# The next block's x is cast in pairs 2 to 5 in place of 0 to 3, and the first two differences of g become one

## The chip, the cores and the metric

One Trainium2 chip, one core of it. The metric is the device time of one execution in microseconds; the median of several runs is compared. TensorE (PE, with its weight loads PEld), VectorE (DVE), ScalarE (ACT), GpSimd (POOL) and SyncE (SP, which here only issues DMAs) each run their own instructions in order, and wait for each other through semaphores. DMAs are issued from two queues: SP's, and GpSimd's own, which also does the transfers that convert a type.

## The reference

```python
def reference(x, w1, w2):          # x 8x1024x1024, w1 1024x4096, w2 4096x1024, float32
    h = x @ w1
    h = 0.5 * h * (1 + np.tanh(np.sqrt(2 / np.pi) * (h + 0.044715 * h ** 3)))
    return (h @ w2).astype(np.float32)
```

## The kernel before, in words

The 8192 tokens are worked through in eight blocks of 1024 (`sb`, 0 to 7). Each block has a first matmul (x times w1, then GELU, which gives g) and a second (g times w2). All operands are float16, and the sums are float32 in PSUM. Both matmuls use a fast scheme of seven products in place of eight: an operand is cut into four blocks "11", "12", "21", "22", sums and differences of the blocks are formed, seven products are made of them (numbers 1 to 7), and their results are added. In blocks 2 to 7 the scheme is used on two levels, so that most products are themselves made of seven smaller ones. This leaves TensorE less to do and VectorE more.

**The first matmul of blocks 2 to 7** is `matmul1_late`. For a block of x, "21" is the second token half and the first half of the hidden dimension. The loop over `j` from 0 to 7 makes one *pair* after another: two chunks of 128 intermediate columns, in each half of g. The four tiles of g are g["11"], g["12"], g["21"] and g["22"], each 128 x 16 x 512, of which pair j fills chunks 2j and 2j + 1. What is done in a pair, and in which order, stands in the list `PAIR` (and `PAIR_FIRST`, `PAIR_LAST`). Every key is one step: `m` and `h` are matmuls (lines 723 and 509), `a`, `p`, `c` copies by ScalarE (line 179), `e`, `f`, `s`, `u`, `z` additions by VectorE (line 152), `g` a GELU by ScalarE (line 522). A key with a prime belongs to the pair before. So the end of pair j - 1 is worked out in pair j, and `d'`, which stands near the end of the list, is step d of the pair before.

- **Step d** (lines 525 to 530 and 769 to 771) replaces g["21"] by g["11"] - g["21"] in the two chunks of its pair: 128 x 1024 float16 values, in place. It runs on GpSimd in pairs 0 to 6 and on VectorE in pair 7 (line 528). What it makes is read in the second matmul.
- **The sums of x** that the inner products need are made on VectorE in float16 (line 368, at line 152 in the profile): at the steps `i` of `PAIR_FIRST`, and in pair 1 at the steps that `X_SUMS` names; the last of these, `i64`, comes after the last key of the list. There are none in later pairs.
- **The weights of a pair** are a `StoredHalf`: six groups (`GROUPS`) that SP loads from DRAM (line 305), as far ahead as the 26 buffers of the pool `up` allow; two halves are there at the start of the stage, and half j + 2 is asked for in pair j. Of halves 3 to 7 the group (s1, s5) isn't loaded; GpSimd makes it in four operations (`make`, line 330) from the group (1, 5), and this stands in GpSimd's order at the start of the pair before.
- **The next block's x** is first converted from float32 to float16, from DRAM to DRAM, into `xb`: `x_cast_paced` (lines 487 to 492). It issues a copy of two columns into a tile `pace` on GpSimd (line 489, called the mark), which waits for a chunk of g and so holds back what follows it, and then two DMAs of 128 rows each on GpSimd's queue (line 484). One call is called a cast pair here. Four of them convert the 1024 rows.
- **Then x is transposed** into four blocks by `x_transpose` (lines 494 to 504): four transposing DMAs a block on SP's queue (`DMA_TRANSPOSE`, line 176), in the order "22", "21", "12", "11", at the ends of pairs 4, 5, 6 and 7. The first two blocks hold the second token half (rows 512 to 1023), the last two the first.

Behind the third transposed block SP issues the first three weight loads of the second matmul (`early.load`, line 815), then the fourth block, then the rest of the second matmul's weights (lines 1011 and 1015). The second matmul's own matmuls have line 1030. At the end of pair 5 GpSimd makes one sum for it (`early.make`, line 1024, 128 x 2048). In its course GpSimd's queue stores the output (line 840).

Blocks 0 and 1 have other code (`matmul1`, `matmul2_made`), which calls `difference` too, on VectorE.

Of the kernel before, what the change touches and what calls it, by code (L numbers as in the profile page):

```python
# [88 lines left out]
def kernel(  # L89
# [7 lines left out]
    nc = tc.nc  # L97
# [10 lines left out]
    NI = I // P // 2  # L108
# [36 lines left out]
    def temp():  # L145
        return tp.tile([P, HT], F32, name="tmp")
# [31 lines left out]
    def act_copy(out, in_):  # L178
        tc.keep_in_program_order(nc.scalar.copy(out=out, in_=in_))  # L179
# [190 lines left out]
    def x_blocks():  # L370
        return {b: unit(KH, HT) for b in ("22", "21", "12", "11")}
# [107 lines left out]
    def x_cast(s, after, rows=range(0, SB, P), xb=None):  # L479
        if xb is None:  # L480
            xb = xdram.tile([SB, H], DT, name="xb")
        with tc.issue_after(after.ins):
            for q in rows:
                nc.gpsimd.dma_start(out=xb[q:q + P, :], in_=x2[s * SB + q:s * SB + q + P, :])
        return xb

    def x_cast_paced(s, g_chunk, q, xb, pin=False):

        mark = nc.gpsimd.tensor_copy(out=pace, in_=g_chunk[:, :2])
        if pin:  # L490
            tc.keep_in_program_order(mark)
        return x_cast(s, mark, range(q * P, (q + 2) * P, P), xb)

    def x_transpose(xb, dma, blocks=None, which=range(4)):
        blocks = blocks or x_blocks()
        for b, t in [list(blocks.items())[i] for i in which]:
            a, k = int(b[0]) - 1, int(b[1]) - 1
            for j in range(KH):
                dma(
                    t[:, j, :],  # L500
                    xb[a * HT:(a + 1) * HT, (k * KH + j) * P:(k * KH + j + 1) * P],
                    transpose=True,
                )
        return blocks
# [13 lines left out]
    def add(out, in1, in0=None):  # L518
        tt(out, out if in0 is None else in0, in1, ADD, True)

    def gelu_into(out, src):
        gelu_last[0] = nc.scalar.activation(out=out, in_=src, func=GELU)  # L522
        tc.keep_in_program_order(gelu_last[0])

    def difference(g, j, engine=nc.vector):
        if j >= 0:
            cs = slice(2 * j, 2 * j + 2)
            tc.keep_in_program_order(engine.tensor_tensor(  # L528
                out=g["21"][:, cs], in0=g["11"][:, cs], in1=g["21"][:, cs], op=SUB,
            ))  # L530
# [4 lines left out]
    def g_tiles():  # L535
        return {b: g_tile(b) for b in ("11", "12", "21", "22")}
# [6 lines left out]
    def matmul1(xs, sb, quads, start=None):  # L543
# [29 lines left out]
        for j in range(NI // 2):  # L573
# [46 lines left out]
            for h in range(2):  # L620
                add(a[h], banks_b[h])
            difference(g, j - 1)
            half = (len(jobs) + 1) // 2
            if start is not None and j == 1:
# [56 lines left out]
    class Pair:  # L681
# [7 lines left out]
        def bank(self, b, h):  # L689
            if (b, h) not in self.banks:  # L690
                self.banks[b, h] = psum()
            return self.banks[b, h]
# [35 lines left out]
        def run(self, key):  # L728
            kind, m, i = key[0], int(key[1:2] or 0), int(key[2:3] or 0)
            bank, temp = self.bank, self.temp  # L730
            if kind == "m" and m in self.whole:
                if i in (1, 4):
                    self.half(m, int(i == 4), m != 6)
            elif kind == "m":
                self.part(m, i)
            elif kind == "h":
                self.half(m, i, False)
            elif kind in "czf" and m in self.whole:
                pass
            elif kind == "c":  # L740
                act_copy(temp("c", m)[:, left], bank("a" if m == 1 else "c", 1)[:, right])
            elif kind == "z" and m in (1, 5):
                b = "a" if m == 1 else "c"
                z = bank(b, 1)[:, left]
                if i == 1:
                    act_copy(bank(b, 0)[:, left], z)
                else:
                    out = bank(b, 0) if i == 2 else bank(b, 1)
                    add(out[:, right], z, temp("c", m)[:, left])
            elif kind == "f":  # L750
                add(temp("q", 0)[:, right if i else left], bank("a", 1)[:, right], temp("a", i)[:, right])
            elif kind in "ez":
                b, t = {2: ("b", "a"), 3: ("d", "s"), 6: ("a", "a")}[m]
                z = bank(b, 1)[:, left]
                if kind == "e":
                    add(temp(t, i)[:, right], bank(b, 1)[:, right])
                else:
                    h, cols = ((0, left), (0, right), (1, right), (1, left))[i - 1]
                    base = temp(t, h)[:, cols]
                    if m == 6 and cols == right:  # L760
                        base = temp("q", 0)[:, right if h else left]
                    add(bank(b, h)[:, cols], z, base)
            elif kind in "ap":
                act_copy(temp(kind, m), bank("a" if kind == "a" else "c", m))
            elif kind == "s":
                add(temp("s", m), bank("a", m), temp("p", m))
            elif kind == "u":
                add(temp("p", m), bank("a", m))
            elif kind == "d":
                spare = self.j < NI // 2 - 1  # L770
                difference(self.g, self.j, nc.gpsimd if spare else nc.vector)
            else:
                b, h = key[1:3], int(key[3])
                src = temp("p", h) if b == "22" else bank({"11": "b", "21": "a", "12": "d"}[b], h)
                gelu_into(self.g[b][:, 2 * self.j + h, :], src)

    def matmul1_late(xs, sb, quads, g):
        n = NI // 2
        nxt = {}
        early = Inner(4, g["22"])  # L780
        made = set(xs.inner)

        def x_sum(key):
            if int(key[1]) not in made:
                xs.inner_sum(int(key[1]), int(key[2]))

        last = None
        for j in range(n + 1):
            if MADE_HALF <= j + 1 < n:
                quads[j + 1].make()  # L790
            if j < n:
                quads += [StoredHalf(i) for i in range(len(quads), min(j + 3, n))]
                now = Pair(j, quads[j], xs, g)
            if j == n:
                for key in PAIR_LAST:
                    last.run(key)
                break
            for key in PAIR if j else PAIR_FIRST:
                if key[0] == "i":
                    x_sum(key)  # L800
                elif key[-1] == "'":
                    last.run(key[:-1])
                else:
                    now.run(key)
                for job in X_SUMS.get(key, ()) if j == 1 else ():
                    x_sum(job)
            last = now
            if sb < NSB - 1:
                if j < 4:
                    after = g["11"][:, 2 * j - 1, :] if j else xs.inner[5][:, 0, 0, :]  # L810
                    nxt["xb"] = x_cast_paced(sb + 1, after, 2 * j, nxt.get("xb"), True)
                if j == 3:
                    nxt["blocks"] = x_blocks()
                if j == n - 1:
                    early.load(STEPS[:3])
                if j > 3:
                    x_transpose(nxt["xb"], load_in_order, nxt["blocks"], range(j - 4, j - 3))
            if j == 5:
                early.make(7, nc.gpsimd, up, "u")
        blocks = nxt.get("blocks")  # L820
        return g, early, None if blocks is None else XOps(blocks)
# [261 lines left out]
    def matmul2(sb, g, early, nxt):  # L1083
# [56 lines left out]
        new, quads = {}, []  # L1140
        products[4].load()
        run((0, 0))
        for m, after in zip(order, order[1:] + (None,)):
            into[m] = into[1] if m == 6 else [claim(), claim()]
# [23 lines left out]
    xs, quads = first.xs, [first.quad]  # L1168
    g_late = None
    for sb in range(NSB):  # L1170
        if sb < 2:
            g, nxt = matmul1(xs, sb, quads, first if sb == 0 else None)
            xs, quads = matmul2_made(sb, g, None if sb else quads[-1].keep_raw, nxt)
            continue
        g, early, nxt = matmul1_late(xs, sb, quads, g_late or g_tiles())
        g_late, quads = matmul2(sb, g, early, nxt)
        xs = nxt
# [30 lines left out]
```

## Time and profile before

| | us |
|---|---|
| median of 3 runs | 1480.92 |
| lowest and highest of them | 1478.4, 1481.01 |
| the profiled execution | 1483.45 |
| its span, from the first to the last instruction | 1481.7 |

The profile is of one execution. In its views a line of a group or of a timeline names the line of the code, the engine, the operation, and the tiles as out<-in; in square brackets, or behind the bar, stands how long the engine was idle before it and what ended that. `ps` is a PSUM bank, `tmp` a float32 tile that ScalarE or VectorE fills from PSUM, `u` and `gc` are tiles of the two pools that hold weights and sums, `g` is g, `w_d` and `in_d` are the prepared weights in DRAM. The wait view has total time, number of times, and the longest. The view of one line or tile ends with how long its DMAs took from issue to landing. Times on GpSimd are rough.

### The profile page before, as it was taken

To read this page: it belongs to the slowest core of one execution; us is meant where nothing else is said; L and a number is where in the kernel's file an instruction comes from. 1 tells how busy PE (TensorE), PEld (TensorE's weight loads), DVE (VectorE), ACT (ScalarE), POOL (GpSimd) and SP (SyncE) were. 2 spreads that over 40 slices of the span, in tenths; PEclk is the share of its full clock that TensorE was granted. 3 is DMA by queue.
4 is the path that set the end of the run, shared out by engine and by line. 5 is a ranking of instruction groups with operands and counts; after the bars stand their busy time and mean duration, and the time that the engine had idled before them with its cause. 6 is when DMAs were issued, how large, how long until landed. Compare 5 with 4: busy or idle time off the path is not lost.

```text
span 1481.7 us, 28425 instructions
## 1 busy us (share of the span) xinstructions
PE 1457.0 (98%) x10635; PEld 1039.1 (70%) x10635; DVE 1264.3 (85%) x2226; ACT 611.1 (41%) x1226; POOL 454.9 (31%) x473
## 2 busy tenths in 40 slices
PE   9999999999989999999999999999999999999998
PEld 5444444444467888678877788777886778867787
DVE  5657468768789999999999999999999999899997
ACT  5665125621157411663126621366214752056510
POOL 1442122223347012560026501274103631136111
PEclk9999999999999999999999999999999999999999
DMA  9999897898999999999999999999999999996896
GB/s 324 338 337 391 234 345 278 309 289 286 362 346 220 349 291 365 352 221 364 302 370 329 211 379 316 363 293 231 383 340 343 290 281 324 352 338 215 319 295 220
DMA packets 205706, 462.86 MB, mean 312 GB/s; under 512 B 75648, under 2 KB 80768, under 8 KB 204672
## 3 DMA queue, kind: packets, MB, share of 16 engines
q1 hardware_dynamic: 177632, 363.52, 73.1%
q0 software_dynamic: 27936, 97.53, 22.0%
q8 instruction: 83, 1.36, 0.4%
q14 instruction: 55, 0.45, 0.1%
HBM read 360.32 MB, written 115.34 MB: 321 GB/s over the span
## 4 chain that ended last, share of the span: by engine, by line
PE 91%; DVE 4%; DMA 3%; POOL 1%; issue 1%; ACT 0%; SPq 0%; DVEq 0%
PE ps L1030 34%; PE ps L509 22%; PE ps L723 20%; PE ps L1071 13%; DMA u<-w_d 3%; DVE gc L152 1%; DVE u L152 1%; PE ps L442 1%; DVE tmp L152 1%; POOL u L330 1%; DVE ps L152 1%; PE ps L419 0%; DMA u<-in_x_dram 0%; PE ps L377 0%; ACT u L179 0%
## 5 line engine op out<-in xcount | busy, mean ns | idle before, releaser
L152 DVE TENSOR_TENSOR tmp<-tmp,ps 128x256 f32<-128x256 f32 (+1 forms) x582 | 311.0, 553 | 90.1 <-PE ps L509 39.5
L509 PE MATMUL ps<-u 128*128 128x512 f16 x1552 | 363.2, 379 | 0.0
L179 ACT COPY tmp<-ps 128x512 f32<-128x512 f32 (+1 forms) x398 | 208.6, 541 | 293.3 <-PE ps L1071 136.6
L152 DVE TENSOR_TENSOR ps<-tmp,ps 128x256 f32<-128x256 f32 x720 | 292.2, 425 | 33.8 <-PE ps L723 24.3
L723 PEld LDWEIGHTS <-u 128*128 128x128 f16 x2688 | 262.5, 98 | 80.4 <-DMA u<-w_d 7.5
L1030 PE MATMUL ps<-u,gc 128*128 128x256 f16 x2592 | 290.8, 273 | 0.0
L1030 PEld LDWEIGHTS <-gc 128*128 128x128 f16 x2592 | 253.6, 98 | 29.4
L509 PEld LDWEIGHTS <-u 128*128 128x128 f16 x1552 | 151.8, 98 | 147.4 <-issue 0.2
L152 DVE TENSOR_TENSOR u<-u 128x512 f16<-128x512 f16 (+3 forms) x316 | 231.2, 774 | 27.5 <-DMA w_d<-u 11.4
L522 ACT ACTIVATE g<-ps 128x512 f16<-128x512 f32 x326 | 188.4, 595 | 99.5 <-PE ps L723 63.9
L1030 PE MATMUL ps<-u,g 128*128 128x256 f16 x2016 | 227.9, 273 | 0.0
L179 ACT COPY u<-ps 128x512 f32<-128x512 f32 (+1 forms) x134 | 78.0, 587 | 354.4 <-PE ps L1030 346.3
L723 PE MATMUL ps<-u 128*128 128x256 f16 x1456 | 220.2, 273 | 0.0
L840 POOL DMA_DIRECT2D out_dram<-u x70 | 63.9, 948 | 487.3 <-DVE u L152 253.4
L1030 PEld LDWEIGHTS <-g 128*128 128x128 f16 x2016 | 197.2, 98 | 22.8
L723 PE MATMUL ps<-gc,u 128*128 128x256 f16 x1232 | 202.7, 273 | 10.4 <-DMA u<-w_d 5.9
L152 DVE TENSOR_TENSOR u<-u,ps 128x512 f32<-128x512 f32 x216 | 147.4, 682 | 36.6 <-PE ps L1030 27.4
L1071 PE MATMUL ps<-u,g 128*128 128x512 f16 x768 | 166.4, 379 | 0.0
L528 POOL TENSOR_TENSOR g<-g,g 128x1024 f16<-128x1024 f16 x42 | 89.4, 2129 | 208.7 <-ACT g L522 208.7
L330 POOL TENSOR_TENSOR u<-u 128x512 f16<-128x512 f16 x120 | 136.3, 1158 | 33.5 <-DMA u<-w_d 13.3
L522 ACT ACTIVATE g<-tmp 128x512 f16<-128x512 f32 x186 | 116.9, 631 | 58.0 <-DVE tmp L152 58.0
L1071 PEld LDWEIGHTS <-g 128*128 128x128 f16 x768 | 75.1, 98 | 90.6
(54 smaller groups left out, 902.4 us busy)
## 6 DMA issues: line engine op xcount, KB each, us to landing
u<-w_d SPq DMA_DIRECT2D x240, 512.0 KB, 8.3
u<-in_d SPq DMA_DIRECT2D x168, 512.0 KB, 8.2
u<-w_d SPq DMA_DIRECT2D x125, 448.0 KB, 10.1
out_dram<-u POOLq DMA_DIRECT2D x70, 512.0 KB, 11.0
gc<-in_w_dram SPq DMA_DIRECT2D x48, 512.0 KB, 6.2
w_d<-u POOLq DMA_DIRECT2D x40, 512.0 KB, 7.8
w_d<-u SPq DMA_DIRECT2D x32, 512.0 KB, 8.6
in_d<-u POOLq DMA_DIRECT2D x28, 512.0 KB, 5.4
```

What stands on the lines that cost most here:

```text
L152: i = nc.vector.tensor_tensor(out=out, in0=in0, in1=in1, op=op)
L179: tc.keep_in_program_order(nc.scalar.copy(out=out, in_=in_))
L330: nc.gpsimd.tensor_tensor(out=operand(j), in0=operand(u), in1=operand(v), op=op)
L442: tc.keep_in_program_order(nc.tensor.matmul(bank[:, cols], lhsT=w[:, k, :], rhs=self.xs.blocks[f"{a}{r}"][:, k, cols], start=r == 1 and k ...
L509: tc.keep_in_program_order(nc.tensor.matmul(bank, lhsT=w, rhs=x, start=first and k == 0, stop=k == n - 1, skip_group_check=not first,))
L522: gelu_last[0] = nc.scalar.activation(out=out, in_=src, func=GELU)
L528: tc.keep_in_program_order(engine.tensor_tensor(out=g["21"][:, cs], in0=g["11"][:, cs], in1=g["21"][:, cs], op=SUB,))
L723: tc.keep_in_program_order(nc.tensor.matmul(out, lhsT=w, rhs=x, start=first and k == 0, stop=k == 1, skip_group_check=not first,))
L840: return nc.gpsimd.dma_start(out=rows, in_=src, **kw)
L1030: tc.keep_in_program_order(nc.tensor.matmul(bank[:, i * OH // 2:(i + 1) * OH // 2], lhsT=t[:, c, i * P:(i + 1) * P], rhs=self.y[j][:, c, : ...
L1071: tc.keep_in_program_order(nc.tensor.matmul(pair(bank), lhsT=a[:, c, :], rhs=chunks(pieces[c // QC])[:, :, c % QC, :], start=(first and c ...
```

## The change

```diff
-    def difference(g, j, engine=nc.vector):
+    def difference(g, j, engine=nc.vector, n=1):
         if j >= 0:
-            cs = slice(2 * j, 2 * j + 2)
+            cs = slice(2 * (j + 1 - n), 2 * j + 2)
...
             elif kind == "d":
-                spare = self.j < NI // 2 - 1
-                difference(self.g, self.j, nc.gpsimd if spare else nc.vector)
+                if self.j == 1:
+                    difference(self.g, 1, nc.gpsimd, 2)
+                elif self.j > 1:
+                    difference(self.g, self.j, nc.gpsimd if self.j < NI // 2 - 1 else nc.vector)
...
             if sb < NSB - 1:
-                if j < 4:
-                    after = g["11"][:, 2 * j - 1, :] if j else xs.inner[5][:, 0, 0, :]
-                    nxt["xb"] = x_cast_paced(sb + 1, after, 2 * j, nxt.get("xb"), True)
+                if 1 < j < 6:
+                    nxt["xb"] = x_cast_paced(sb + 1, g["11"][:, 2 * j - 1, :], 2 * j % 8, nxt.get("xb"), True)
```

Step d of pair 0 is left out, and step d of pair 1, which runs in pair 2, does the four chunks of both pairs in one operation of 128 x 2048. This holds for blocks 2 to 7.

The cast pairs at the ends of pairs 0, 1, 2 and 3, for rows 0, 256, 512 and 768 onward, become cast pairs at the ends of pairs 2, 3, 4 and 5, for rows 512, 768, 0 and 256 onward. So those of the second token half stay where they were, and those of the first token half come four pairs later. This holds for blocks 2 to 6; block 7 has no next x. The transposes, and every order but GpSimd's, are as before. In GpSimd's order a cast pair now stands between the difference and the sums of the next half in pairs 4 and 5, and none does in pairs 0 and 1.

## The prediction

> **What bounds the kernel now.** I read the page's engine row first, then busy time by stage, then TensorE's waits, then the timeline around each wait, and last the DMAs behind it.
>
> ```profile
> span 1481.7 us, 28425 instructions
> PE 1457.0 (98%) x10635; PEld 1039.1 (70%) x10635; DVE 1264.3 (85%) x2226; ACT 611.1 (41%) x1226; POOL 454.9 (31%) x473
> ```
>
> TensorE sets the end: it is idle for 1481.7 - 1457.0 = 24.7 us, and no edit that leaves its matmuls alone can bring more. By stage (columns: stretch, length, then busy time and count of PE, PEld, DVE, ACT, POOL, clock, DMA share, GB/s), the first matmul of block 3, then its second:
>
> ```profile
> 582.10:677.50 95.40, 92.26 (x688) 66.79 (x687) 89.42 (x218) 60.20 (x122) 47.62 (x42) 1.00 0.97 291
> 677.50:761.40 83.90, 83.90 (x771) 75.21 (x769) 77.37 (x92) 14.22 (x35) 9.44 (x10) 1.00 1.00 351
> ```
>
> The idle time lies in the first matmul (3.1 us here) and none in the second. What TensorE waited for, with total, times and longest:
>
> ```profile
> PE ps L723 <- DVE tmp L152: 6.1, 4, 2.0
> PE ps L723 <- DMA u<-w_d: 5.9, 4, 2.2
> PE ps L723 <- POOL u L330: 4.3, 3, 2.9
> ...
> PE ps L723 <- DMA g<-w_d: 1.1, 1, 1.1
> ```
>
> The rest is start and tail. All four rows are line 723, the inner products of the first matmul in blocks 2 to 7. The fullest case of the first row, end of pair 1 in block 4:
>
> ```profile
> 778.40 0.42 DVE L152 TENSOR_TENSOR gc<-u 128x512 f16<-128x512 f16 x1
> ...
> 779.31 2.11 POOL L528 TENSOR_TENSOR g<-g,g 128x1024 f16<-128x1024 f16 x1 [12.10 <-ACT g L522]
> 779.40 2.30 DVE L152 TENSOR_TENSOR gc<-u,gc 128x512 f16<-128x512 f16 x1
> ...
> 781.62 0.41 DVE L152 TENSOR_TENSOR tmp<-tmp,ps 128x256 f32<-128x256 f32 x1
> ...
> 782.08 0.38 PE L723 MATMUL ps<-u,g 128*128 128x256 f16 x2 [2.03 <-DVE tmp L152]
> ```
>
> GpSimd's first difference of g starts at 779.31. The last x sum of pair 1, begun 0.09 us later on VectorE, takes 2.30 us in place of 0.42; the add queued behind it comes at 781.62, and TensorE stands 2.03 us for that add.
>
> The other kind, block 3: the group (s1, s5) of pair 1's weights, who waited for it, and the first cast pair of the next x:
>
> ```profile
> L305 SPq DMA_DIRECT2D u<-w_d x1: 320/320/320, 580.7 to 580.7; - x1
> ...
>   PE ps L723: 2.1, 1
> ...
> DMA to landing us min/median/max: 21.5/21.5/21.5
> ```
>
> ```profile
> L484 POOL DMA_DIRECT2D xb<-in_x_dram x2: 515/523/531, 586.9 to 587.4; - x2
> ...
> DMA to landing us min/median/max: 13.6/14.1/14.6
> ```
>
> The weights land at 580.7 + 21.5 = 602.2, the casts at 586.9 + 13.6 = 600.5 and 587.4 + 14.6 = 602.0: all three arrive in the same 2 us, and TensorE waits 2.1 us. GpSimd afterwards:
>
> ```profile
> 600.01 2.11 POOL L528 TENSOR_TENSOR g<-g,g 128x1024 f16<-128x1024 f16 x1 [12.10 <-ACT g L522]
> ...
> 602.39 1.01 POOL L484 DMA_DIRECT2D xb<-in_x_dram  x2
> 610.65 4.61 POOL L330 TENSOR_TENSOR u<-u 128x512 f16<-128x512 f16 x4 [7.25 <-DMA u<-w_d]
> ```
>
> Here the sums of half 3 (line 330) wait 7.25 us for a weight group behind both cast pairs, and end just as pair 3 wants them: the POOL row of the waits. The difference runs at 600.01 in this block too, where the DMA wait hides it.
>
> **The change, part by part.** *The first difference leaves pair 1.* No other GpSimd operation stands in pair 1 now except a mark and casts, which leave too. So the three DVE waits (6.1 in four, three of them near 2.0; I take 5.9) go, and so does the same stall under the DMA waits of the other three blocks. Price: one operation of twice the size, a pair later.
>
> ```profile
> L528 POOL TENSOR_TENSOR g<-g,g 128x1024 f16<-128x1024 f16 x42 | 89.4, 2129 | 208.7 <-ACT g L522 208.7
> ...
> L1024 POOL TENSOR_TENSOR u<-g 128x2048 f16<-128x2048 f16 x6 | 24.4, 4073 | 0.0
> ```
>
> 128x2048 is not in the trace for a difference, but line 1024's has that size: 4.07 us, bounded by 2 x 2.13 = 4.26. It adds 1.95 to 2.13 us behind d of pair 1. Queued there: a mark, two casts, the sums of the next half. Would VectorE suffer in its new place? A difference in block 2, beside what VectorE does there:
>
> ```profile
> 436.29 2.13 POOL L528 TENSOR_TENSOR g<-g,g 128x1024 f16<-128x1024 f16 x1
> 436.36 1.33 DVE L152 TENSOR_TENSOR ps<-tmp,ps 128x256 f32<-128x256 f32 x3 [3.60 <-PE ps L723]
> ```
>
> 1.33 / 3 = 0.44 us each, unhurt: outside pair 1 VectorE only adds from PSUM here, and its order is unchanged. So I cost it at nothing; if one of the x sums stood there, it would be up to 4.1 us a block. The sums of half 3, no longer queued behind casts, start at 610.65 - 5.6 = 605.0 at the earliest in block 3; the x sum that follows the release of 600.01 by 0.1 us is over by then.
>
> The Trainium skill (SBUF — State Buffer, Who interferes with whom) says that a DVE instruction with two SBUF inputs and a GpSimd one that reads SBUF lock each other out for the whole instruction, and that one with a single SBUF input does not contend. Both rows above agree. By that rule a doubled difference is a doubled hold, which speaks against the merge wherever a two-input operation follows it.
>
> *The casts go from pairs 0 and 1 to pairs 4 and 5.* Rows 512 to 1023, cast after pairs 2 and 3, stay. What two casts cost the weights: the two above land 1.5 us apart in a full queue, 3.1 us for both; alone, eight in a row:
>
> ```profile
> L484 POOL DMA_DIRECT2D xb<-in_x_dram x8: 493/502/527, 151.1 to 154.5; - x8
> ...
> DMA to landing us min/median/max: 7.9/11.1/14.1
> ```
>
> First landing 151.1 + 7.9 = 159.0, last 154.5 + 14.1 = 168.6: 9.6 / 7 = 1.4 each, 2.8 for two. If the weights would get half the engines in that time anyway, they gain only 1.5. I take 2.8 from the first pair, as the landing of 602.2 shows little progress beside the casts, and 5.6 from both. Needed are 2.2, 2.1 and 1.3 us (the DMA row's 5.9, less 0.3 early in block 2) in blocks 2, 3 and 5, and, for the POOL waits behind them, at most 2.2 + 2.9 = 5.1. All is covered: 5.6 + 4.3 = 9.9 us go. At the low price 0.7 and 0.6 of the first waits stay and up to 1.4 more of the longest POOL wait (5.1 needed, 3.0 given): 2.7 left. The 1.1 of the g row lies before any cast and stays.
>
> *What the casts meet in pairs 4 and 5.* On GpSimd the sums of half 7 come 1.1 us later (a mark and 1.01 of issue):
>
> ```profile
> 825.81 2.12 POOL L528 TENSOR_TENSOR g<-g,g 128x1024 f16<-128x1024 f16 x1 [4.40 <-ACT g L522]
> 827.89 4.07 POOL L1024 TENSOR_TENSOR u<-g 128x2048 f16<-128x2048 f16 x1
> 831.91 4.63 POOL L330 TENSOR_TENSOR u<-u 128x512 f16<-128x512 f16 x4
> 836.90 2.12 POOL L528 TENSOR_TENSOR g<-g,g 128x1024 f16<-128x1024 f16 x1 [0.36 <-ACT g L522]
> ```
>
> They end at 836.54; pair 7 begins near 836.9, where the end of pair 6 releases the next difference, and it needs three of the four sums first, done at 835.4. 1.5 of room less 1.1: nothing, or 0.2 us in five blocks if the issue is slow. On SP the third x block (first token half) must now wait for the casts of pair 5:
>
> ```profile
> 826.23 10.95 SPq L176 DMA_TRANSPOSE u<-xb  x8
> ...
> 845.91 1.00 SPq L1011 DMA_DIRECT2D u<-in_d  x2
> ```
>
> ```profile
> L484 POOL DMA_DIRECT2D xb<-in_x_dram x56: 486/512/642, 151.1 to 1163.2; - x56
> ...
> DMA to landing us min/median/max: 5.7/7.4/14.6
> ```
>
> The third block begins about 826.2 + 5.5 = 831.7; the casts, behind the difference that ends at 827.93, would be issued from 828.0 to 829.0 and land at the median 7.4 later, 835.9: SP stands 4.2 us. Behind it are four transposes, three early weight loads, four transposes, then the loads from 845.91. The second of these two has the least room:
>
> ```profile
> L1011 SPq DMA_DIRECT2D u<-in_d x1: 376/376/376, 846.5 to 846.5; - x1
> ...
> DMA to landing us min/median/max: 7.0/7.0/7.0
> ```
>
> ```profile
> 862.29 1.91 PE L1030 MATMUL ps<-u 128*128 128x256 f16 x16
> ```
>
> Landed 853.5, read 862.3: 8.8 us of room against 4.2. Nothing. TensorE's earlier arrival moves SP and GpSimd with it.
>
> *The clock.* In block 7:
>
> ```profile
> 1316.00:1317.50 1.50, 0.58 (x6) 0.52 (x6) 1.50 (x5) 0.00 (x0) 0.25 (x1) 1.00 1.02 388
> 1317.50:1321.10 3.60, 3.60 (x21) 2.60 (x19) 2.45 (x7) 1.24 (x3) 3.20 (x3) 0.53 1.03 408
> ```
>
> Right after that block's DVE wait the clock is 0.53 for 3.6 us: 1.7 us lost. Of six such blocks only this has it, and I can't tell whether the unprofiled runs do; it stays out of the sum and bounds it below.
>
> The Trainium skill (TensorE: Matmul & The Clock Gate, What's actually happening) has the clock halve after an idle window of about 3.4 us. The wait here was some 2.0, so the row differs; by the rule the dip is no result of this wait and stays, by the row it may go, 1.7 us more.
>
> *Sum.* 5.9 + 9.9 = 15.8 us. The profiled execution took 1483.45 us, 1.75 around its span; it becomes 1467.65. The median of the three runs, 1480.92, becomes 1465.1, forecast 1465. Low bound 1480.9 - 15.8 - 1.7 = 1463.4, high 1480.9 - 15.8 + 2.7 + 1.0 = 1468.8.
>
> **The rivals.**
> - *Only the DVE waits go (0.12).* For it: weights take up to 21.5 us to land, and the stores of the block before share their queue. Against: three rows of landing in 2 us. 1480.9 - 5.9 = 1475.
> - *SP is the new bound, at the start of the second matmul (0.11).* Should the pair-5 casts land like the slowest, 14.6 us, SP stands 11.4 and the load with 8.8 of room is 2.6 late, in five blocks: 13 us, 1478. From 15.1 us of latency on, 3.1 x 5 eats the whole gain; beyond 15.7 it is slower. For it: the transposes share the engines with these casts, which they never did. Against: 14.6 is a cast behind stores, and no stores are due here. Slower side 0.06, about 1486 at 16.2 us.
> - *The doubled difference catches VectorE (0.04).* As in pair 1, but 4.1 - 0.4 = 3.7 us in six blocks, 22 us against 15.8: 1487. The order of VectorE speaks against it.
> - *It does nothing (0.04).* Other loads come late at the same spots: 1480.
>
> **How the numbers follow.** Forecast 0.69, with its own range 1463 to 1469. The range 1462.5 to 1474 adds the partial cases on the way to 1475. A measurement here can't tell less than 0.2%, 3 us. Faster: 0.69 + 0.12 + 0.03 of SP = 0.84. Same: 0.02 + 0.04 = 0.06. Slower: 0.06 + 0.04 = 0.10.
>
> **What would show it.** Right: no PE wait for DVE near 2 us, no VectorE x sum over 0.5 us in pair 1, six differences of 128x2048 near 4.1 us, PE idle in the first matmul under 1 us a block but for the 1.1, and the second matmul still without idle. Wrong: waits for DMA of u<-w_d left in blocks 2, 3, 5 (the relief), a wait on line 1030 (SP), or POOL line 330 at pair 7 (the mark and casts).

## The result, and the profile after

| | median, us | lowest to highest | runs |
|---|---|---|---|
| before | 1480.88 | 1478.05 to 1481.71 | 7 |
| after | 1468.98 | 1464.43 to 1473.23 | 7 |

The ratio is 0.9922, with a 95% interval of 0.9903 to 0.9942: faster by 11.9 us, inside the range, 4 us above the forecast. The runs of after spread over 8.8 us, those of before over 3.7. The profiled execution of after is its slowest (1473.23), so what went wrong can be seen in it. Its page:

```profile
span 1471.5 us, 28413 instructions
PE 1455.3 (99%) x10635; PEld 1036.7 (70%) x10635; DVE 1255.5 (85%) x2226; ACT 610.8 (42%) x1226; POOL 451.4 (31%) x467
```

TensorE's idle time is 1471.5 - 1455.3 = 16.2 us, 8.5 less than before; its busy time is 1.7 less. What it waited for (total, times, longest):

```profile
PE ps L723 <- DMA g<-w_d: 4.1, 2, 2.2
PE ps L1031 <- DMA u<-in_d: 2.7, 2, 2.4
PE ps L419 <- DVE tmp L411: 2.0, 3, 1.1
```

The three rows that the sum removes (DVE 6.1, u<-w_d 5.9, POOL 4.3) are gone, each of them whole. Two others are there: waits at line 1031 (line 1030 of before), the second matmul, which had none, and 4.1 us in place of 1.1 for the first weights of a block. The row of line 419 (0.8 in before) lies in the first 25 us of the kernel, which the change leaves alone. By stage, the first matmul of block 3 and the second of block 4 (columns as before):

```profile
577.00:671.30 94.30, 91.96 (x688) 66.85 (x686) 87.69 (x218) 60.05 (x122) 47.20 (x41) 1.00 1.02 281
...
847.00:934.00 87.00, 84.32 (x772) 75.02 (x771) 77.56 (x93) 14.57 (x36) 9.46 (x10) 1.00 1.02 361
```

Of the 2.3 us idle in the first of these, 2.18 are one wait, where pair 1 begins; in the second, 2.7 us are idle where before had no idle time.

The timeline of pair 1 in block 4, where TensorE had stood 2.03 us: the last x sum on VectorE takes 0.41 us now (2.30 before). The second row is the doubled difference, a pair later:

```profile
773.33 0.41 DVE L152 TENSOR_TENSOR gc<-u,gc 128x512 f16<-128x512 f16 x1
...
784.57 4.06 POOL L528 TENSOR_TENSOR g<-g,g 128x2048 f16<-128x2048 f16 x1 [0.45 <-ACT g L522]
```

**Where the new wait of the second matmul comes from.** SP's timeline in block 4; its first row is the second and the third x block (in before it read 826.23, 10.95 us for the eight transposes):

```profile
818.37 22.63 SPq L176 DMA_TRANSPOSE u<-xb  x8
...
843.84 6.22 SPq L176 DMA_TRANSPOSE u<-xb  x4
850.16 1.00 SPq L1012 DMA_DIRECT2D u<-in_d  x2
```

The eight take 22.63 us, since SP stands before the third x block. The view of tile xb in the microsecond in which the casts of pair 5 were issued (it holds one transpose too):

```profile
L484 POOL DMA_DIRECT2D xb<-in_x_dram x2: 486/505/524, 820.0 to 820.6; - x2
...
DMA to landing us min/median/max: 12.9/15.3/16.6
```

The 16.6 us are the transpose's. The two casts took 12.9 and 15.3, where the prediction took 7.4, and SP goes on at 836.0, when the second has landed (820.6 + 15.3 = 835.9). In the other four blocks these casts took 7.4 to 11.1. What SP waited for, over blocks 2 to 6 (before has no such row), then from 820 to 845, in block 4:

```profile
SPq L176 <- DMA xb<-in_x_dram: 26.8, 13, 7.5
```

```profile
SPq L176 <- DMA xb<-in_x_dram: 8.6, 2, 5.8
```

The two loads behind it, issued at 850.2 and 850.8, are the ones that TensorE waits for; the view of their line, then TensorE's timeline:

```profile
L1012 SPq DMA_DIRECT2D u<-in_d x2: 376/453/530, 850.2 to 850.8; - x2
...
  PE ps L1031: 2.7, 2
...
DMA to landing us min/median/max: 4.9/5.7/6.5
```

```profile
855.21 1.91 PE L1031 MATMUL ps<-u,gc 128*128 128x256 f16 x16 [2.45 <-DMA u<-in_d]
857.34 1.92 PE L1031 MATMUL ps<-u 128*128 128x256 f16 x16 [0.23 <-DMA u<-in_d]
```

850.2 + 4.9 = 855.1 and 850.8 + 6.5 = 857.3, just when TensorE goes on. Without the 8.6 us the second load would have landed at 848.7, and it was wanted at 857.34 - 0.23 - 2.45 = 854.66: 6.0 us of room, and 8.6 - 6.0 = 2.6 is the wait. So the room is 6.0 and not the 8.8 read from before: TensorE comes 7.6 us earlier (854.66 against 862.29) and the transposes start 7.9 earlier (818.37 against 826.23), as forecast, but without the stand the eight still take 22.63 - 8.6 = 14.0 us and not 10.95. The stand alone does not make a wait. In block 2 SP stood 8.0 us for these casts, and no load came late, since its eight transposes take 18.59 - 8.0 = 10.6 without the stand:

```profile
464.04 18.59 SPq L176 DMA_TRANSPOSE u<-xb  x8
```

**Where the wait at the start of block 3 comes from** is less clear. Its traces lead up to 100 us upstream. The stretch in which block 2's last transposes and the second matmul's loads are in flight, and the end of that matmul (columns as before; the last two are the share of the DMA engines and GB/s):

```profile
470.00:490.00 20.00, 20.00 (x153) 14.77 (x152) 18.93 (x48) 13.11 (x26) 9.61 (x7) 1.00 0.81 139
490.00:510.00 20.00, 20.00 (x174) 16.86 (x173) 18.36 (x28) 7.46 (x17) 0.00 (x0) 1.00 1.03 329
...
530.00:546.00 16.00, 16.00 (x149) 14.32 (x148) 14.34 (x16) 3.49 (x9) 2.49 (x2) 1.00 1.05 326
```

The same stretches of the kernel of experiment 6, which has no cast in pair 5 and no wait there:

```profile
470.00:490.00 20.00, 20.00 (x153) 14.79 (x152) 19.03 (x50) 13.25 (x27) 7.73 (x6) 1.00 0.93 198
490.00:510.00 20.00, 20.00 (x178) 17.16 (x176) 18.37 (x26) 6.84 (x17) 0.00 (x0) 1.00 1.02 393
...
530.00:546.00 16.00, 16.00 (x149) 14.35 (x147) 13.97 (x15) 2.77 (x7) 1.81 (x2) 1.00 0.99 260
```

After moves (198 - 139 + 393 - 329) x 20 us = 2.5 MB less up to 510, and more than the other from 530 to 546 (326 against 260 GB/s). The stores of the output lie in that crowd, and SP, which has to reuse their buffer, waits for one of them. That wait in after, then in the kernel of experiment 6:

```profile
SPq L1012 <- DMA out_dram<-u: 4.7, 1, 4.7
```

```profile
SPq L1012 <- DMA out_dram<-u: 1.8, 1, 1.8
```

The next block's first weights stand behind it on SP. The group that TensorE waits for, (s1, s5) of pair 1, and TensorE's timeline:

```profile
L305 SPq DMA_DIRECT2D g<-w_d x1: 320/320/320, 568.3 to 568.3; - x1
...
  PE ps L723: 2.2, 1
...
DMA to landing us min/median/max: 16.6/16.6/16.6
```

```profile
584.94 0.39 PE L723 MATMUL ps<-gc,g 128*128 128x256 f16 x2 [2.18 <-DMA g<-w_d]
```

568.3 + 16.6 = 584.9. In the kernel of experiment 6 the same load goes out at 565.9 and lands 11.7 us later, at 577.6. Of the 7.3 us between the two landings, 2.4 are the later issue, which the store wait can explain, and 4.9 the longer flight, which it can't.

Store waits and late starts go together in several profiles: waits of 4.7 and 5.0 us in blocks 2 and 4 of after are followed by 2.18 and 1.96 at the next start, 4.1 in the second profile by 2.49, 4.8 and 4.2 in experiment 8 by 3.01 and 1.16. But not in all: 4.1 in experiment 4 and 3.9 in experiment 7 are followed by none, five of 4.2 to 5.1 in experiment 5 by 0.91 at most (there the waits at line 1031 hold TensorE back), and before has 1.11 at the start of block 5 behind one of 1.6. Experiment 4 also moves 2.4 MB less than experiment 6 up to 510, and its block 3 begins without a wait. So it is shown, by experiments 6 and 10, that this wait goes when no cast stands in pair 5; the steps between the casts and the late load are read from traces laid side by side, and stay open.

### The profile page after: what moved, and what is told of

The parts are those of the page before. It is cut to its first block, busy times and chain, and to the rows that moved or that the text cites. A ratio compares the mean times of both kernels' runs of the same rounds, so it can differ in the third digit from the quotient of the medians.

```text
span 1471.5 us, 28413 instructions
## 1 busy us (share of the span) xinstructions
PE 1455.3 (99%) x10635; PEld 1036.7 (70%) x10635; DVE 1255.5 (85%) x2226; ACT 610.8 (42%) x1226; POOL 451.4 (31%) x467
## 4 chain that ended last, share of the span: by engine, by line
PE 65%; DVE 3%; DMA 3%; issue 1%; DVEq 0%
PE ps L1031 33%; PE ps L723 21%; PE ps L509 11%; DMA g<-w_d 2%; DVE tmp L152 1%; DVE gc L152 1%; DVE u L152 1%; DVE ps L152 1%; DMA u<-in_d 0%; DVEq L152 0%
## 5 line engine op out<-in xcount | busy, mean ns | idle before, releaser
L152 DVE TENSOR_TENSOR u<-u 128x512 f16<-128x512 f16 (+3 forms) x316 | 231.2, 774 | 28.3 <-DMA w_d<-u 11.1
L528 POOL TENSOR_TENSOR g<-g,g 128x1024 f16<-128x1024 f16 (+1 forms) x36 | 88.1, 2448 | 107.7 <-ACT g L522 107.7
```

The lines of the kernel that those rows point to most:

```text
L152: i = nc.vector.tensor_tensor(out=out, in0=in0, in1=in1, op=op)
L528: tc.keep_in_program_order(engine.tensor_tensor(out=g["21"][:, cs], in0=g["11"][:, cs], in1=g["21"][:, cs], op=SUB,))
```

## The experiments

Diffs are against the changed kernel. Ratios are to the kernel before, run beside each of them; the expectations name their theories themselves.

**1. The changed kernel again**, a second profile.

> The changed kernel once more, for a second profile. Theory A (the waits that are new come from SP standing at the third x block until pair 5's casts have landed): the casts of pair 5 land 7 to 16 us after their issue from block to block, and the new waits at the start of the second matmul and of the next block differ from the first profile; 1464 to 1473 us. Theory B (the new waits come from TensorE arriving earlier at weights that land no earlier): the same two waits of near 2 us at the start of blocks 3 and 5, and 1469 within 2.

Measured 1466.41 (1464.40 to 1472.86), ratio 0.9906 [0.9879, 0.9933]; its profiled execution has a span of 1466.4. One wait is left, with SP's row below it:

```profile
PE ps L723 <- DMA g<-w_d: 2.5, 1, 2.5
```

```profile
SPq L176 <- DMA xb<-in_x_dram: 18.8, 9, 5.1
```

In block 4 the last two cast pairs land after 6.6 to 8.4 us this time, SP does not stand at all for them, and the second matmul has no wait. The program is the same, so how long the pair-5 casts take differs from one execution to the next, and the time with it. All eleven runs of this program, of the result and of this one, have a median of 1468.1.

**2. The difference alone**, with the casts back in pairs 0 to 3:

```diff
-                if 1 < j < 6:
-                    nxt["xb"] = x_cast_paced(sb + 1, g["11"][:, 2 * j - 1, :], 2 * j % 8, nxt.get("xb"), True)
+                if j < 4:
+                    after = g["11"][:, 2 * j - 1, :] if j else xs.inner[5][:, 0, 0, :]
+                    nxt["xb"] = x_cast_paced(sb + 1, after, 2 * j, nxt.get("xb"), True)
```

> The merged difference alone, casts in pairs 0 to 3 as before. Theory A: the two parts add up. The three DVE waits (5.9 us) are gone, the DMA and POOL waits in pairs 1 to 3 stay at about 9.9 us, and nothing new comes at the second matmul: 1475 us. Theory B: TensorE, now earlier, waits longer for the same weights; waits for DMA grow by what the DVE waits lose: 1479 to 1481.

Measured 1487.45 (1486.46 to 1490.22), ratio 1.0043 [1.0028, 1.0059]: slower than before, by 6 us, which no theory had. Waits of its profile, and GpSimd's timeline in block 3:

```profile
PE ps L723 <- DMA u<-w_d: 14.0, 4, 4.9
...
PE ps L723 <- POOL u L330: 1.6, 1, 1.6
```

```profile
587.52 1.04 POOL L484 DMA_DIRECT2D xb<-in_x_dram  x2
595.00 0.18 POOL L489 COPY pace<-g 128x2 f16<-128x2 f16 x1 [6.44 <-ACT g L522]
595.45 0.96 POOL L484 DMA_DIRECT2D xb<-in_x_dram  x2 [0.26 <-issue]
```

The second cast pair goes out at 595.45; in before it was 602.39, behind the difference at 600.01. The mark of that pair waits for chunk 1 of g["11"] only, which is there early. What had held the casts back until then was the difference, which stood ahead of the mark in GpSimd's order and waited for g["21"]. So it paced the casts: the two pairs now follow each other in 7.9 us, where before had 15.5 (586.9 to 602.39). The clock adds to it: in this profile it is at half speed for some 17 us in three places. For 13.4 of them TensorE was at work, which costs some 6.7 us; the others lie in its waits.

**3. The same with the pace restored:** the mark of the second pair waits for g["21"], as the difference did.

```diff
-                if 1 < j < 6:
-                    nxt["xb"] = x_cast_paced(sb + 1, g["11"][:, 2 * j - 1, :], 2 * j % 8, nxt.get("xb"), True)
+                if j < 4:
+                    after = (xs.inner[5][:, 0, 0, :], g["21"][:, 1, :], g["11"][:, 3, :], g["11"][:, 5, :])[j]
+                    nxt["xb"] = x_cast_paced(sb + 1, after, 2 * j, nxt.get("xb"), True)
```

> The merged difference with the casts in pairs 0 to 3 as before, but the mark of pair 1 waits for the last GELU of pair 0 (chunk 1 of g 21), as the difference of pair 0 that stood ahead of it did. Theory C (the difference of pair 0 held the second cast pair back; without it the casts of pair 1 are issued some 8 us earlier, ahead of weights): casts of pair 1 near 421, 602, 782 again, the DMA and POOL waits back to about 9.9 us, the DVE waits gone, no clock dips after the first matmuls of pairs 1: 1475 us. Rival (TensorE, earlier by the DVE waits, runs into weights that land no earlier): DMA waits of 14 us or more as in the merged difference alone, 1481 to 1487.

Measured 1476.69 (1474.57 to 1478.13), ratio 0.997 [0.9957, 0.9983]. In block 3 the second cast pair goes out at 598.33, and what is left is the two rows for which the casts are to blame, with no wait near 2 us for VectorE:

```profile
PE ps L723 <- POOL u L330: 5.5, 5, 2.1
...
PE ps L723 <- DMA u<-w_d: 3.5, 3, 1.5
```

The lost pace is what made experiment 2 slow: the two differ in one operand of a mark, and in 1487.45 - 1476.69 = 10.8 us, dips of the clock included.

**4. The casts alone**, with the differences as in before:

```diff
-                if self.j == 1:
-                    difference(self.g, 1, nc.gpsimd, 2)
-                elif self.j > 1:
-                    difference(self.g, self.j, nc.gpsimd if self.j < NI // 2 - 1 else nc.vector)
+                spare = self.j < NI // 2 - 1
+                difference(self.g, self.j, nc.gpsimd if spare else nc.vector)
```

> The later casts alone, the differences as before. Theory A: no PE wait for DMA u<-w_d in pairs 1 to 3, but a wait for DVE near 2.0 us in each of the six blocks, 12 in all, since it is no longer hidden under a DMA wait: 1477 to 1481 us, about no change. Rival: the casts carry the gain by themselves, and the DVE waits are hidden elsewhere: 1471.

Measured 1478.43 (1475.91 to 1484.31), ratio 0.9986 [0.9973, 0.9999]. The waits for casts are nearly gone, and the stalls in pair 1 have come out from under them, five in place of three (four near 2 us and one of 0.99, behind a wait of 0.87; the sixth wait of the row is 0.17 and lies elsewhere):

```profile
PE ps L723 <- DVE tmp L152: 9.2, 6, 2.0
...
PE ps L723 <- DMA u<-w_d: 0.9, 1, 0.9
```

Theory A has the time right and the count wrong: block 5 has no stall. There VectorE's x sum starts at 954.47 and takes 0.42 us, and the difference, which starts at 954.51, takes 2.37 in place of 2.13. In before block 5 is the same (958.05 and 958.09). Wherever VectorE was held, in before and in experiments 4 and 9, the difference had started first, by 0.03 to 0.17 us.

**5. The casts a pair later still**, in pairs 3 to 6: this makes SP's stand longer.

```diff
-                if 1 < j < 6:
-                    nxt["xb"] = x_cast_paced(sb + 1, g["11"][:, 2 * j - 1, :], 2 * j % 8, nxt.get("xb"), True)
+                if 2 < j < 7:
+                    nxt["xb"] = x_cast_paced(sb + 1, g["11"][:, 2 * j - 1, :], (2 * j - 2) % 8, nxt.get("xb"), True)
```

> The suspected cost enlarged: casts in pairs 3 to 6 (rows 512, 768, 0, 256 onward), so that the third x block waits for casts that are issued 11 us later. Theory A: SP stands 15 us or more there, the weights of the second matmul come late in all five blocks by 5 us or more each: 1490 us or above, with waits on line 1031. Theory B: SP has room, no such waits: 1464 to 1470.

Measured 1499.52 (1494.74 to 1504.13), ratio 1.0122 [1.0094, 1.0149]: 18 us slower than before.

```profile
PE ps L1031 <- DMA u<-in_d: 13.2, 6, 3.0
...
PE ps L1031 <- DMA u<-w_d: 2.6, 4, 1.5
```

The wait is the one that after shows in block 4, now in all five blocks that cast. Its size a block, 2.5 to 4.1 us, is below what was expected. Other waits came with it, 4.4 us for GpSimd's sums (line 330), 1.9 for an x sum and 1.9 for the first weights of a block, and clock dips beside three of the waits add to the time.

**6. No cast in pair 5:** three cast pairs are out by the end of pair 3, and the last goes out in pair 4.

```diff
-                if 1 < j < 6:
-                    nxt["xb"] = x_cast_paced(sb + 1, g["11"][:, 2 * j - 1, :], 2 * j % 8, nxt.get("xb"), True)
+                for q in {2: (4,), 3: (6, 0), 4: (2,)}.get(j, ()):
+                    nxt["xb"] = x_cast_paced(sb + 1, g["11"][:, 2 * j - 1, :], q, nxt.get("xb"), True)
```

> The change, with the first half's rows cast after pairs 3 and 4 in place of 4 and 5 (pair 3 issues two cast pairs). Theory A (the new waits come from SP standing at the third x block): SP stands under 2 us there, no wait at the start of the second matmul, and the waits for g<-w_d at the start of blocks 3 and 5 fall under 0.5 us: 1464 to 1466, and less spread than the change. Theory B (weights that simply land no earlier): the waits for g<-w_d of near 2 us stay, 1467 to 1469.

Measured 1464.64 (1464.19 to 1465.26), ratio 0.9888 [0.9871, 0.9904]: its four runs spread over 1.1 us, near the fastest of after's eleven (1464.40). Its page, its largest wait in blocks 2 to 7, and SP's timeline in block 4:

```profile
span 1462.8 us, 28413 instructions
PE 1454.1 (99%) x10635; PEld 1038.1 (71%) x10635; DVE 1253.3 (86%) x2226; ACT 611.1 (42%) x1226; POOL 452.4 (31%) x467
```

```profile
PE ps L723 <- DVE tmp L152: 1.1, 7, 0.2
```

```profile
818.64 13.14 SPq L176 DMA_TRANSPOSE u<-xb  x8
```

The eight transposes start at the same time as in after and take 13.14 us in place of 22.63. No wait for a DMA or for GpSimd is left in these blocks, and the two kernels differ in the casts alone: 1468.98 - 1464.64 = 4.3 us in the median is what the late ones give back (1.8 by the median of experiment 1, 3.5 by all eleven runs). Theory B falls: TensorE arrives earlier still, and the waits are gone.

**7. The last two cast pairs both in pair 4:** `{2: (4,), 3: (6,), 4: (0, 2)}` in that place.

> The change, with both cast pairs of the first half after pair 4. Theory A: their last landing is some 11 us after issue, about when SP comes to the third x block, so SP stands 0 to 3 us, and as in the variant done by pairs 3 and 4 the new waits go: 1464 to 1467. The sums of half 6 come 1 us later, with 5.5 us of room: nothing. Theory B: 1467 to 1469.

Measured 1467.48 (1465.24 to 1468.64), ratio 0.9905 [0.989, 0.9919]. SP stands 1.2 us in all, and neither new wait is there, but its profile has another:

```profile
PE ps L723 <- DMA u<-w_d: 2.9, 2, 2.3
```

2.34 of it is at 408.75, in the first pair of block 2, before any cast that this edit moves in that block. Whether the edit has to do with it stays open.

**8. The weights first:** the early loads of the second matmul go ahead of the third x block on SP, in place of behind it (and in block 7, which has no next x, stay).

```diff
-                if j == n - 1:
+                if j == n - 2:
...
+            if sb == NSB - 1 and j == n - 1:
+                early.load(STEPS[:3])
```

> The change with its casts, but SP issues the first three weight loads of the second matmul ahead of the third x block, in place of behind it. Theory A: SP still stands 3 to 10 us at the third block; the first three weights no longer wait for it, but the next four still do: a wait at the start of the second matmul where SP stands 8 us or more, and the waits at the start of the next block stay: 1466 to 1470, as the change.

Measured 1469.12 (1464.54 to 1470.86), ratio 0.9913 [0.9893, 0.9933]: no better than after. In this profile the second matmul has no wait, but the next blocks' first weights do, and the store wait of block 2 is there too:

```profile
PE ps L723 <- DMA g<-w_d: 4.5, 3, 3.0
```

```profile
SPq L1014 <- DMA out_dram<-u: 4.8, 1, 4.8
```

SP's stand in block 2 is only 2.3 us here, and the start of block 3 is still 3.01 us late. So putting three loads first does not cure the second cost. That the time which casts and transposes take from the DMA engines has to be worked off later, wherever the loads stand, would fit; no run here shows it by itself.

**9. The differences in their own places**, with the casts of experiment 6:

```diff
-                if self.j == 1:
-                    difference(self.g, 1, nc.gpsimd, 2)
-                elif self.j > 1:
-                    difference(self.g, self.j, nc.gpsimd if self.j < NI // 2 - 1 else nc.vector)
+                difference(self.g, self.j, nc.gpsimd if self.j < NI // 2 - 1 else nc.vector)
```

> Casts after pairs 2, 3 (two) and 4, the differences as before the change (that of pair 0 in pair 1). If the difference in pair 1 is worth what VectorE loses to it, and no weights come late: a wait for DVE of 2.0 us in each of the six blocks, 12.0 us over the variant with the merged difference: 1476 to 1478, with a clock dip of 1.7 us in some of the runs. Rival (part of the wait is hidden elsewhere): 1471 to 1474.

Measured 1479.0 (1476.26 to 1479.93), ratio 0.9982 [0.9973, 0.9991]; 14.4 us over experiment 6. All six blocks have the stall, five of 2.04 us and one of 1.97. Below the row, the windows of the stall in block 3 and what follows it:

```profile
PE ps L723 <- DVE tmp L152: 12.2, 6, 2.0
```

```profile
598.00:600.00 2.00, 1.35 (x13) 1.20 (x13) 1.97 (x7) 0.06 (x1) 0.00 (x0) 0.98 1.04 408
600.00:603.40 3.40, 3.40 (x18) 2.28 (x16) 2.73 (x6) 1.40 (x3) 2.03 (x2) 0.51 1.02 411
```

12.2 of waits, 1.1 less of experiment 6's own, and two stretches at half clock (1.7 us lost in each) make 14.5.

**10. Place without merge:** with the casts of experiment 6, step d of pairs 0 and 1 both run in pair 2, as two operations.

```diff
                 if self.j == 1:
-                    difference(self.g, 1, nc.gpsimd, 2)
-                elif self.j > 1:
+                    difference(self.g, 0, nc.gpsimd)
+                if self.j > 0:
                     difference(self.g, self.j, nc.gpsimd if self.j < NI // 2 - 1 else nc.vector)
```

> The same casts, the differences of pairs 0 and 1 both in pair 2 but as two operations of 128x1024. If the place and not the merge does it: 2 x 2.13 = 4.26 us on GpSimd in place of near 4.1, no wait for DVE, 1464 to 1465.5. Rival (one long operation matters): over 1467.

Measured 1464.6 (1464.49 to 1465.33), ratio 0.9892 [0.9876, 0.9909], the same as experiment 6. What counts is that the difference left pair 1; that two became one is worth nothing that can be measured.

## Why the prediction came out as it did

**Right: what goes.** The sum of 15.8 us holds when nothing is given back: it leads from 1480.9 to 1465.1, and experiment 6 has 1464.64. The mechanism of the first term is shown by experiments 6 and 9, which differ in nothing but the differences, and that of the second by 3 and 6, which differ in nothing but the casts. The doubled difference takes 4.06 us (bound 4.07 to 4.26) and hurts no one, and the sums of half 7 make no wait.

**Right in sum, not in the shares.** With the other part in place, the difference is worth 14.4 us (experiments 9 and 6) and the casts 12.1 (3 and 6), against 5.9 and 9.9; alone they bring, by the ratios, 4.4 (3, with the pace kept) and 2.7 (9). Both stalls lie one behind the other in pairs 1 and 2 of the same blocks, and where one goes the other comes out. The prediction said that the stall of pair 1 is hidden under the DMA wait in three blocks, and counted neither twice, which is why the whole comes out. It is two blocks, 2 and 3; in block 5 of before VectorE went first, and there was no stall to hide. The price of the rival "only the DVE waits go", 1475, is close to experiment 3, 1476.7, where the casts stay early; in the change itself its condition fails, since the waits for u<-w_d went too.

**Wrong: "What the casts meet in pairs 4 and 5", and its "Nothing".** Both sizes were off. The latency was put at 7.4 us, the median over casts that had never met a transpose; beside the transposes it was 12.9 and 15.3 in block 4, and SP stood 8.6 us and not 4.2. The room was put at 8.8 and was 6.0; SP did move with TensorE, as the step says, but its eight transposes take 14.0 us in place of 10.95 even without the stand. Most of that is not the pair-5 casts' doing: the eight take 13.14 in experiment 6, where the last cast has landed before they start. By the prediction's own signs this step is wrong: there is a wait on line 1030 (1031 now), and the second matmul has idle time. The step did list the sharing of engines, but in the rival "SP is the new bound", and set it aside because no stores were due there. That rival is what happened in part: 2.7 us in one block of this profile and none in the second one, where its price assumed 2.6 in all five.

**Wrong: "The 1.1 of the g row ... stays".** It is a wait for weights that SP issues at the end of the second matmul, and the prediction took it as out of the change's reach. It is 4.1 us in two blocks of this profile and zero in experiment 6, so the casts of pair 5 do reach it. The way there, over slow transposes, loads in a crowd and a late store, is argued and not shown. This second half of the price was in no rival.

**Missed: what the difference held back.** The change moved an operation that paced the second cast pair. Moved together the parts hide it; experiments 2 and 3 put it at 10.8 us. The prediction shows that the difference waits for a GELU and that casts stand behind it, and drew nothing from it.

**The clock** stayed out of the sum, and its low bound was not reached. Each profile of before and after has one dip, at 1317.6 and at 942.1, so nothing is gained between these two. Experiments 6 and 10 have none.

## What to carry to other kernels

Before an operation is moved, ask what stands behind it in its engine's order and was held back by it; if that is a DMA, give it a wait of its own. Price a moved DMA with what is in flight at its new place, not with the median of its old ones. A load queue that falls behind can pay later: look for the bill in the next stage's first loads too.

## What the runs showed of the hardware

- *Little was moved while casts and transposes were in flight together.* In block 4 of after the pair-5 casts run beside transposes. The windows from there on:

```profile
815.00:825.00 10.00, 10.00 (x79) 7.55 (x78) 9.24 (x25) 7.19 (x15) 7.13 (x5) 1.00 1.22 287
825.00:836.00 11.00, 11.00 (x87) 8.39 (x86) 10.24 (x27) 7.84 (x16) 6.72 (x6) 1.00 1.24 80
```

  The engines show full shares, 1.24 (the packets of one engine overlap in the records), and carry 80 GB/s in the second window. Eight transposes without casts beside them went with 210 GB/s at a share of 1.02 in before (826 to 837) and 220 at 1.05 in experiment 6 (821 to 832). Part of that is weights: SP, standing, issued no load in the window of after. How much is the casts', and why, isn't shown.

- *The clock halves after waits of about 2 us, though not after each.* A dip behind such a wait is 3.4 us long and costs 1.7. It followed a wait of 1.96 in after (but not those of 2.18 and 2.45), of 2.49 in the second profile, of 1.97 in experiment 4 (but not three of 2.04), and two of six waits in experiment 9; the one of 2.34 in experiment 7 brought none. Waits of 4.13 and 4.91 in experiment 2 had the clock down for some 7 us, part of it in the wait. The two profiles without a wait of 1.9 us or more, experiments 6 and 10, have none before their tails. The Trainium skill (TensorE: Matmul & The Clock Gate, What's actually happening) asks for an idle window of about 3.4 us; these rows show shorter ones, and the measurement decides. So a wait of 2 us costs between 2.0 and 3.7.
